# A hybrid attention trunk on one core: rows copied to all partitions by DRAM transfers instead of selector matmuls

## The chip, the cores and the metric

The program runs on one core of a Trainium2 chip. The metric is the device time of one execution in microseconds (us). The engines are PE (TensorE; PEld is its weight load), DVE (VectorE), ACT (ScalarE), POOL (GpSimd) and SP (SyncE, which here only issues DMA transfers). Each engine works through its own queue in order and waits for semaphores of the others.

## What is computed

Two layers of a trunk on a sequence of 1024 tokens of width 1024, all in float32. Each layer normalises its input, projects it (`h @ w_in`, 9180 columns) and runs three branches on the result: sparse attention (DSA, the best 256 keys of each query by an index score, 8 heads), stick-breaking attention (8 heads) and a chunked mLSTM (4 heads of 128). The gated sum of the branches goes through `w_out` and is added to the input.

Two pieces matter here. The first is the decays of the mLSTM (reduced from the reference):

```python
b = jnp.cumsum(lfb, axis=-1)
log_d = jnp.where(tril, b[..., :, None] - b[..., None, :] + ib[..., None, :], -jnp.inf)
log_inter = b + m_prev[..., None]
m_row = jnp.maximum(jnp.max(log_d, axis=-1), log_inter)
w_intra = jnp.exp(log_d - m_row[..., None])
w_inter = jnp.exp(log_inter - m_row)
s = jnp.einsum('bhtd,bhsd->bhts', qb, kb) * w_intra
num = einsum(s, vb) + w_inter * einsum(qb, c_mem)
c_mem = decay * c_mem + einsum(w_upd, kb, vb)
```

The second is the keys of DSA: of the 64 entries of a key the first 16 are the rotated `k_rope`, the same for all heads, and the other 48 are `c_kv @ w_uk`.

## The kernel before

`body` (L614) does not issue instructions but logs them. `Plan.run` then sets every engine's order by simulating the program with a table of costs (L82 to 91, `cost`), buffers and priorities, and `Plan.emit` issues the instructions in that order at L533, which is why all rows of the profile name that line. A small edit in `body` can therefore move rows anywhere. Buffers of 520 or 1032 columns per partition (classes `half`, 21, and `slab`, 35; two halves may share a slab) and eight PSUM banks are handed out by the planner too. In rows, `t` is a buffer, `s` one that lies in a shared slab, `d` a DRAM buffer.

A float32 product is three passes of F32R matmuls over a high and a low part of each operand (`PASSES`). A layer runs in this order: projections and index scores; the mLSTM; the stick-breaking attention; DSA; the merge. Two things run beside it. The merge gates (`AHEAD`, L1038) are projected early and fill PE between other work, in the buffers `fill` and PSUM banks `psf`. The top-k search (`tk_bit`) is a chain of 32 rounds, put between other steps by `tick` (L944). A round (`count`, L951) counts over six score tiles: DVE does the tiles of 384, 512 and 640 columns, ACT those of 768, 896 and 1024, and three small DVE operations on 128x6 make the next threshold out of the six counts.

The mLSTM works on chunks of 128 tokens, 4 heads (`h`), two halves (`th`) of four chunks each. Heads 0 and 2 project values and gates for two heads and are longer. For a head, PE transposes the keys, and DVE multiplies them by the update weights into `kw` (L1200 to 1207). Then for each half:

- `selm(h)` (L1212) is a matmul with a column of `sel_ml`, copied along the free axis, as the stationary operand and `pk[th]` as the moving one. `pk[th]` holds high and low parts of eight rows (decay `rr_`, inter-chunk weight `wi`, four heads each); the product adds the two parts of one row and copies it to all 128 partitions. The next matmul (L1213) adds the causal mask `m_ml` in bf16. ACT takes the exponential with a bias per partition, from PSUM.
- PE multiplies keys and queries, DVE multiplies the product by the exponential into `Wt`.
- `selm(4 + h)` (L1225) copies the row `wi` to all partitions; DVE multiplies the queries by it into `qs`.
- For each chunk PE computes `Wt` x values and adds `qs` x state; from `kw` x values (128x129, two passes of float32) and the old state DVE makes the new state, with the factor `dec` (L1249).

The rows of `pk` are written to DRAM and read back in another layout (L1116 to 1128). `dec` (L1134 to 1140) is made by 8 four-column selector matmuls per layer.

In DSA, `dsa_k` (L1465) computes the keys of a pair of heads, 128x512 for each half: three passes `w_uk` x `c_kv` with zeros in the 16 rotary rows, and a fourth matmul (L1478) that adds the rotary rows with the selector `sel_kr` and the tile `krs[th]`, which is loaded from `kr_d` once per layer. `stack_k` (L1291) splits the result into high and low parts, two tiles per half (ACT casts, DVE subtracts, 64x512 each). `logits` (L1384) uses them.

Of the kernel before, what the change touches and what calls it, by code (L numbers as in the profile page):

```python
# [613 lines left out]
def body(log, tiles, caps, x_in, w_in, w_uk, w_uv, kvn, conv_w, ib, fb, mln, w_br, w_out, nrm, fnrm,  # L614
# [50 lines left out]
    sel_kr = const([128, 128], F32R, "sel_kr")  # L665
    zer = const([128, 48], F32, "zer")
    V.memset(zer, 0.0)
    for e in range(2):
        V.tensor_tensor(sel_kr[:, 64 * e:64 * e + 16], ident[:, 0:16], ident[:, 16:32], ALU.add)
        V.tensor_copy(sel_kr[:, 64 * e + 16:64 * e + 64], zer)  # L670
    sel_ml = const([128, 8], F32R, "sel_ml")
    for j in range(8):
        k = (j % 4) + 8 * (j // 4)
        V.tensor_tensor(sel_ml[:, j:j + 1], ident[:, k:k + 1], ident[:, k + 4:k + 5], ALU.add)
# [10 lines left out]

    def selm(j):
        return sel_ml[:, j:j + 1].to_broadcast([128, 128])
# [109 lines left out]
    for l in range(DEPTH):  # L797
# [317 lines left out]
        hl = half(F32R)  # L1115
        pkd = dram([4, 32, 128], F32R)  # L1116
        for q, src in ((0, rr_), (2, wi)):
            split(src, hl[0:32, q * 128:q * 128 + 128], hl[0:32, q * 128 + 128:q * 128 + 256])
        for q in range(4):
            SY.dma_start(f(pkd[q]), f(hl[0:32, q * 128:q * 128 + 128]))  # L1120
        pk = []
        for th in range(2):
            k = half(F32R)
            pk.append(k)
            G.memset(f(k[:, :512]), 0.0)
            for q in range(4):
                SY.dma_start(f(k[4 * q:4 * q + 4, :512]).rearrange("h (c t) -> h c t", c=4),
                             f(pkd[q, 16 * th:16 * th + 16, :]).rearrange("(c h) t -> h c t", h=4))
# [5 lines left out]
        pd = pst("tr")  # L1134
        for h in range(4):
            for th in range(2):
                PE.matmul(pd[:, h * 8 + th * 4:h * 8 + th * 4 + 4], selm(4 + h),
                          pk[th][:, 127:512:128], start=True, stop=True)
        dec = small([128, 4, 8], name="dec", bufs=1)
        V.tensor_copy(dec, pd[:, 0:32].rearrange("p (h c) -> p h c", h=4))  # L1140
# [3 lines left out]
        for h in range(4):  # L1144
# [63 lines left out]
            Cst = None  # L1208
# [224 lines left out]


        ckh, ckl = [], []
        krs = []
        for th in range(2):
            c = half()
            SY.dma_start(c[:, :512], ckvT_d[:, th * 512:th * 512 + 512])
# [265 lines left out]
```

## Time and profile before

| what | us |
|---|---|
| time, median of 3 runs | 2734.28 |
| lowest and highest of the 3 | 2730.94, 2734.89 |
| the profiled execution's own time | 2734.7 |
| its span, from first to last instruction | 2732.9 |
| PE busy | 2690.6 |
| DVE, ACT, POOL busy | 1670.8, 1474.7, 1109.0 |

A group row of the profile gives count, busy time, mean length of one and the idle time ahead of it with what ended that. Matmuls overlap, so the price of one is the distance from start to start, which a merged timeline row gives as its length by its count. A timeline row merges neighbouring rows and bears the shape of the first. The wait in square brackets is idle time ahead of the first instruction of the row.

### The profile page before, as it was taken

To read this page: it belongs to the slowest core of one execution; us is meant where nothing else is said; L and a number is where in the kernel's file an instruction comes from. 1 tells how busy PE (TensorE), PEld (TensorE's weight loads), DVE (VectorE), ACT (ScalarE), POOL (GpSimd) and SP (SyncE) were. 2 spreads that over 40 slices of the span, in tenths; PEclk is the share of its full clock that TensorE was granted. 3 is DMA by queue.
4 is the path that set the end of the run, shared out by engine and by line. 5 is a ranking of instruction groups with operands and counts; after the bars stand their busy time and mean duration, and the time that the engine had idled before them with its cause. 6 is when DMAs were issued, how large, how long until landed. Compare 5 with 4: busy or idle time off the path is not lost.

```text
span 2732.9 us, 43639 instructions
## 1 busy us (share of the span) xinstructions
PE 2690.6 (98%) x15658; PEld 2306.7 (84%) x15666; DVE 1670.8 (61%) x3964; ACT 1474.7 (54%) x2961; POOL 1109.0 (41%) x1481
## 2 busy tenths in 40 slices
PE   8999999999999999999899999999999999999998
PEld 7888878888888888889898888888888888888898
DVE  5828788666686663424447287896676776624244
ACT  4637763545567766512236277735555577764131
POOL 4323333334253433455433233442342444334654
PEclk9999999999999999999999999999999999999999
DMA  4302112112132215745313022122121322246462
GB/s 131 97 16 80 37 57 83 39 55 82 31 103 61 78 54 177 243 143 206 104 41 109 24 62 62 51 67 66 39 74 33 102 64 77 61 167 231 161 206 77
DMA packets 251149, 249.53 MB, mean 91 GB/s; under 512 B 22378, under 2 KB 201908, under 8 KB 250932
## 3 DMA queue, kind: packets, MB, share of 16 engines
q1 hardware_dynamic: 250932, 246.75, 28.5%
q8 instruction: 123, 2.02, 0.3%
q14 instruction: 94, 0.77, 0.1%
HBM read 184.37 MB, written 62.32 MB: 90 GB/s over the span
## 4 chain that ended last, share of the span: by engine, by line
PE 52%; ACT 3%; DVE 2%; issue 1%; DMA 1%; POOL 1%; SPq 0%; POOLq 0%; DVEq 0%; ACTq 0%
PE t L533 52%; ACT t L533 2%; DVE t L533 1%; POOL t L533 1%; ACT s L533 1%; DMA d<-t 0%; DMA t<-in_w_in_dram 0%; ACT L533 0%; DVE s L533 0%; SPq L533 0%; DMA t<-d 0%; POOLq L1701 0%; DVEq L533 0%; ACTq L533 0%; POOLq L533 0%
## 5 line engine op out<-in xcount | busy, mean ns | idle before, releaser
L533 PE MATMUL t<-t,t 128*128 128x512 f32 (+5 forms) x15466 | 2669.2, 336 | 34.7 <-DVE t L533 29.2
L533 PEld LDWEIGHTS t<-t,t 128*128 128x128 f32 x15330 | 2271.0, 184 | 394.9 <-DVE t L533 41.2
L533 POOL TENSOR_TENSOR t<-t,t 128x256 fp32r<-128x256 f32 (+4 forms) x1092 | 875.7, 830 | 1178.8 <-ACT t L533 470.9
L533 DVE TENSOR_TENSOR t<-t,t 128x512 f32<-128x512 f32 (+14 forms) x1514 | 757.4, 532 | 691.0 <-ACT t L533 498.3
L533 ACT CAST t<-t 128x512 fp32r<-128x512 f32 (+6 forms) x1073 | 563.9, 569 | 520.3 <-PE t L533 238.7
L533 ACT ACTIVATE t<-t 128x512 f32<-128x512 f32 (+4 forms) x704 | 350.8, 593 | 339.6 <-PE t L533 216.3
L533 ACT ACTIVATE t<-t,t 128x768 bf16<-128x768 f32 (+10 forms) x352 | 279.1, 813 | 26.4 <-DVE t L533 18.3
L533 ACT COPY t<-t 64x256 f32<-64x256 f32 (+4 forms) x294 | 109.4, 377 | 267.1 <-PE t L533 262.9
L533 DVE TENSOR_TENSOR_SCAN t<-t 128x256 f32<-128x256 f32 (+10 forms) x144 | 210.5, 1473 | 6.5 <-ACT t L533 6.2
L533 DVE SCALAR_TENSOR_TENSOR t<-t,t,t 128x512 f32<-128x512 f32 (+8 forms) x214 | 162.3, 777 | 28.4 <-DMA d<-t 11.6
L533 POOL TENSOR_SCALAR t<-t 64x512 fp32r<-64x512 f32 x128 | 85.1, 666 | 194.2 <-ACT t L533 157.7
L533 ACT ACT_TABLE_LOAD x111 | 142.4, 1283 | 25.9 <-PE t L533 13.4
L533 POOL TENSOR_SCALAR t<-t,t 128x256 f32<-128x256 f32 (+7 forms) x128 | 95.4, 754 | 138.4 <-DVE t L533 126.1
L533 DVE TENSOR_SCALAR_CACHE_REDUCE t<-t,t 128x512 bf16<-128x512 f32 (+2 forms) x173 | 128.3, 768 | 0.9
L533 DVE TENSOR_TENSOR s<-s,t 128x512 f32<-128x512 f32 x70 | 51.5, 737 | 96.3 <-PE t L533 96.2
L533 DVE CUSTOM_DVE_ANT_0 t<-t,t 128x512 f32<-128x512 f32 (+3 forms) x160 | 92.6, 591 | 20.9 <-PE t L533 17.6
L533 DVE TENSOR_SCALAR t<-t 128x1 f32<-128x1 f32 (+5 forms) x324 | 59.1, 188 | 24.0 <-ACT t L533 21.6
L533 PE MATMUL t<-s,t 128*128 128x512 f32 (+1 forms) x192 | 62.3, 379 | 0.0
L533 DVE RECIPROCAL t<-t 128x1 f32<-128x1 f32 (+1 forms) x144 | 23.0, 163 | 56.1 <-ACT t L533 55.2
L533 DVE TENSOR_TENSOR t<-t 128x1 f32<-128x1 f32 (+9 forms) x234 | 53.0, 238 | 4.7 <-POOL t L533 2.3
L533 ACT ACTIVATION_READ_ACCUMULATOR t<-t,t 128x1 f32 x280 | 52.9, 189 | 0.0
L533 ACT ACTIVATE s<-t,t 128x896 bf16<-128x896 f32 (+2 forms) x40 | 41.6, 1041 | 15.0 <-DVE s L533 14.5
(37 smaller groups left out, 417.4 us busy)
## 6 DMA issues: line engine op xcount, KB each, us to landing
t<-in_w_in_dram SPq DMA_DIRECT2D x192, 256.0 KB
d<-t SPq DMA_DIRECT2D x134, 256.0 KB
t<-d SPq DMA_DIRECT2D x128, 256.0 KB
t<-in_w_in_dram SPq DMA_DIRECT2D x44, 512.0 KB
s<-d SPq DMA_DIRECT2D x76, 256.0 KB
d<-t SPq DMA_DIRECT2D x130, 128.0 KB
t<-in_w_branch_dram SPq DMA_DIRECT2D x32, 512.0 KB
t<-in_w_out_dram SPq DMA_DIRECT2D x32, 512.0 KB
```

Of the source, the lines that this page charges most:

```text
L533: fn(*args, **kw)
```

## The change

- The mLSTM's rows `rr_` and `wi` go to DRAM as they are (two stores of 32x128 in place of four stores of high and low parts). For each head and half, two transfers (`row`) read a row of 4 x 128 values from there into all 128 partitions, 512 bytes a piece, 256 KB a transfer; 32 in the two layers.
- GpSimd adds the mask `m_ml` to the decay row, two operations of 128x256 for each head and half. ACT takes the exponential from this row. DVE multiplies the queries by the other row, from SBUF instead of PSUM. The state's decay is the last column of each chunk in that row; `dec` is gone.
- DSA's keys are computed by three passes, and `stack_k` splits them without the rotary part. Then four transfers of 16x512 for each pair and half write the rotary rows' high and low parts from `kr_d` into the two tiles. `krs` and its memsets are gone.
- The selectors `sel_ml`, `sel_kr` and their set-up are gone.

```diff
--- before.py
+++ after.py
@@ -662,16 +662,6 @@
     cs = const([128, NB, 16], F32, "cs")
     neghalf = const([128, 1], F32, "neghalf")
     V.memset(neghalf, -0.5)
-    sel_kr = const([128, 128], F32R, "sel_kr")
-    zer = const([128, 48], F32, "zer")
-    V.memset(zer, 0.0)
-    for e in range(2):
-        V.tensor_tensor(sel_kr[:, 64 * e:64 * e + 16], ident[:, 0:16], ident[:, 16:32], ALU.add)
-        V.tensor_copy(sel_kr[:, 64 * e + 16:64 * e + 64], zer)
-    sel_ml = const([128, 8], F32R, "sel_ml")
-    for j in range(8):
-        k = (j % 4) + 8 * (j // 4)
-        V.tensor_tensor(sel_ml[:, j:j + 1], ident[:, k:k + 1], ident[:, k + 4:k + 5], ALU.add)
...
-
-    def selm(j):
-        return sel_ml[:, j:j + 1].to_broadcast([128, 128])
 
...
@@ -1112,32 +1099,23 @@
         S.activation(wi, rr_, AF.Exp, bias=mpc)
         S.activation(wu, ii, AF.Exp, bias=rr_[:, 127:128])
         S.activation(en, ml, AF.Exp, scale=-1.0)
-        hl = half(F32R)
-        pkd = dram([4, 32, 128], F32R)
-        for q, src in ((0, rr_), (2, wi)):
-            split(src, hl[0:32, q * 128:q * 128 + 128], hl[0:32, q * 128 + 128:q * 128 + 256])
-        for q in range(4):
-            SY.dma_start(f(pkd[q]), f(hl[0:32, q * 128:q * 128 + 128]))
-        pk = []
-        for th in range(2):
-            k = half(F32R)
-            pk.append(k)
-            G.memset(f(k[:, :512]), 0.0)
-            for q in range(4):
-                SY.dma_start(f(k[4 * q:4 * q + 4, :512]).rearrange("h (c t) -> h c t", c=4),
-                             f(pkd[q, 16 * th:16 * th + 16, :]).rearrange("(c h) t -> h c t", h=4))
+        row_d = dram([2, 32, 128])
+        for q, src in enumerate((rr_, wi)):
+            SY.dma_start(row_d[q], src)
+
+        def row(q, h, th):
+
+            r = half()
+            a = row_d[q, 16 * th + h:16 * th + h + 1, :]
+            SY.dma_start(r[:, :512].rearrange("p (c t) -> p c t", c=4),
+                         bass.AP(tensor=a.tensor, offset=a.offset, ap=[[0, 128], [512, 4], [1, 128]]))
+            return r
+
         p = pst("tr")
         for q, src in enumerate((ii, wu, en)):
             PE.transpose(p[:, q * 32:q * 32 + 32], src, ident[:32, :32])
         mlc = small([128, 3, 8, 4], name="mlc", bufs=1)
         V.tensor_copy(mlc.rearrange("p q c h -> p (q c h)"), p[:, 0:96])
-        pd = pst("tr")
-        for h in range(4):
-            for th in range(2):
-                PE.matmul(pd[:, h * 8 + th * 4:h * 8 + th * 4 + 4], selm(4 + h),
-                          pk[th][:, 127:512:128], start=True, stop=True)
-        dec = small([128, 4, 8], name="dec", bufs=1)
-        V.tensor_copy(dec, pd[:, 0:32].rearrange("p (h c) -> p h c", h=4))
 
...
@@ -1206,25 +1184,26 @@
                                 mlc[:, 1, th * 4:th * 4 + 4, h, None].to_broadcast([128, 4, 128]), ALU.mult)
                 kw.append(k)
             Cst = None
+            rows_ = []
+            for th in range(2):
+                r = row(0, h, th)
+                pool_tt(r, r, m_ml.rearrange("p a b -> p (a b)"), ALU.add, 512)
+                rows_.append((r, row(1, h, th)))
             tick(2)
             for th in range(2):
-                p = pst("lg")
-                PE.matmul(p, selm(h), pk[th][:, :512], start=True, stop=False)
-                PE.matmul(p, identb, m_ml.rearrange("p a b -> p (a b)"), start=False, stop=True)
+                rrow, wrow = rows_[th]
                 Wt = half()
                 for t in range(4):
                     c = th * 4 + t
-                    S.activation(Wt[:, t * 128:t * 128 + 128], p[:, t * 128:t * 128 + 128], AF.Exp,
+                    S.activation(Wt[:, t * 128:t * 128 + 128], rrow[:, t * 128:t * 128 + 128], AF.Exp,
                                  bias=mlc[:, 0, c, h:h + 1])
                 p = pst("lg")
                 for t in range(4):
                     PE.matmul(p[:, t * 128:t * 128 + 128], cv[1, th][:, t * 128:t * 128 + 128],
                               cv[0, th][:, t * 128:t * 128 + 128], start=True, stop=True)
                 V.tensor_tensor(Wt[:, :512], Wt[:, :512], p, ALU.mult)
-                p = pst("lg")
-                PE.matmul(p, selm(4 + h), pk[th][:, :512], start=True, stop=True)
                 qs = half()
-                V.tensor_tensor(qs[:, :512], cv[0, th][:, :512], p, ALU.mult)
+                V.tensor_tensor(qs[:, :512], cv[0, th][:, :512], wrow[:, :512], ALU.mult)
                 NUM = half()
                 nv = NUM[:, :516].rearrange("p (t c) -> p t c", t=4)
                 for t in range(4):
@@ -1246,7 +1225,8 @@
                         if c == 0:
                             V.tensor_copy(Cn, p[:, :129])
                         else:
-                            V.scalar_tensor_tensor(Cn, Cst, dec[:, h, c:c + 1], p[:, :129], ALU.mult, ALU.add)
+                            V.scalar_tensor_tensor(Cn, Cst, wrow[:, t * 128 + 127:t * 128 + 128], p[:, :129],
+                                                   ALU.mult, ALU.add)
                         Cst = Cn
...
@@ -1433,7 +1413,6 @@
 
 
         ckh, ckl = [], []
-        krs = []
         for th in range(2):
             c = half()
             SY.dma_start(c[:, :512], ckvT_d[:, th * 512:th * 512 + 512])
@@ -1441,11 +1420,6 @@
             split(c[:, :512], hi, lo)
             ckh.append(hi)
             ckl.append(lo)
-            k = half(F32R)
-            G.memset(f(k[:, :512]), 0.0)
-            for q in range(2):
-                SY.dma_start(f(k[16 * q:16 * q + 16, :512]), f(kr_d[q, :, th * 512:th * 512 + 512]))
-            krs.append(k)
...
@@ -1474,9 +1448,13 @@
             for th in range(2):
                 p = pst("mm")
                 for i, (a, b) in enumerate(PASSES):
-                    PE.matmul(p, uw[:, 128 * a:128 * a + 128], ck[b][th][:, :512], start=(i == 0), stop=False)
-                PE.matmul(p, sel_kr, krs[th][:, :512], start=False, stop=True)
-                r["k"].append(stack_k(p))
+                    PE.matmul(p, uw[:, 128 * a:128 * a + 128], ck[b][th][:, :512], start=(i == 0), stop=(i == 2))
+                k = stack_k(p)
+                for e in range(2):
+                    for q in range(2):
+                        o = 64 * (e ^ q)
+                        SY.dma_start(f(k[e][o:o + 16, :512]), f(kr_d[q, :, th * 512:th * 512 + 512]))
+                r["k"].append(k)
             return r
 
         def dsa_v(pr):
```

**DVE at head 0 of the first layer.** The second layer reads the same. The 128x384, 128x512 and 128x640 rows are a round of counts; the two TENSOR_TENSOR that read `t_1602` (before) and `t_1588` (after) make `kw`. Before:

```order
L533 TENSOR_SCALAR s_2263,t_2264<-t_1025,t_2261 128x384 [waits DMAHW4_49,DMAHW1_49,DMAHW7_49,DVE_49,Pool_49]
L533 TENSOR_SCALAR s_2272,t_2264<-t_1067,t_2261 128x512 [waits PE_49]
L533 TENSOR_TENSOR t_2283<-t_2270,t_1602 128x512 [waits PE_49]
L533 TENSOR_TENSOR t_2279<-t_2279,t_2213 128x512 [waits Activation_49]
L533 TENSOR_TENSOR t_2296<-t_2277,t_1602 128x512 [waits PE_49]
L533 TENSOR_SCALAR s_2306,t_2264<-t_1108,t_2261 128x640 [waits Activation_49]
```

After:

```order
L533 TENSOR_SCALAR s_2224,t_2225<-t_1009,t_2217 128x384 [waits DMAHW2_49,DMAHW0_49,DMAHW3_49,DVE_49,Pool_49]
L533 TENSOR_SCALAR s_2231,t_2225<-t_1051,t_2217 128x512 [waits DMAHW4_49,DMAHW1_49,PE_49]
L533 TENSOR_SCALAR s_2242,t_2225<-t_1092,t_2217 128x640 [waits DVE_49,Activation_49]
L533 TENSOR_TENSOR t_2256<-t_2240,t_1588 128x512 [waits DMAHW1_49,PE_49]
L533 TENSOR_TENSOR t_2254<-t_2254,t_2180 128x512 [waits DMAHW6_49,Activation_49]
L533 TENSOR_TENSOR t_2271<-t_2248,t_1588 128x512 [waits PE_49]
```

The count over 640 columns, which waits for ACT, stood behind both products of `kw` and now stands ahead of both.

**DVE at head 2 of the first layer**, the same steps. Before:

```order
L533 TENSOR_SCALAR s_3857,t_3858<-t_1025,t_3854 128x384 [waits DMAHW2_49,DVE_49,PE_49]
L533 TENSOR_SCALAR s_3864,t_3858<-t_1067,t_3854 128x512 [waits PE_49]
L533 TENSOR_SCALAR s_3873,t_3858<-t_1108,t_3854 128x640 [waits DVE_49,Activation_49]
L533 TENSOR_TENSOR t_3886<-t_3870,t_1602 128x512 [waits PE_49]
L533 TENSOR_TENSOR t_3884<-t_3884,t_3809 128x512 [waits Activation_49]
L533 TENSOR_TENSOR t_3897<-t_3877,t_1602 128x512 [waits PE_49]
```

After:

```order
L533 TENSOR_SCALAR t_3821,t_3822<-t_1009,t_3816 128x384 [waits DVE_49]
L533 TENSOR_TENSOR t_3801<-t_3801,t_3662 128x512 [waits Activation_49]
L533 TENSOR_SCALAR t_3837,t_3822<-t_1051,t_3816 128x512
L533 TENSOR_TENSOR t_3849<-t_3829,t_1588 128x512 [waits DVE_49,PE_49]
L533 TENSOR_TENSOR t_3842<-t_3842,t_3775 128x512 [waits DMAHW0_49,Activation_49,Pool_49]
L533 TENSOR_TENSOR t_3869<-t_3834,t_1588 128x512 [waits PE_49]
```

Here the count over 640 columns stood ahead of `kw` and now stands behind it (it follows five rows on). In head 2 of the second layer, where before the rows stood as in the first layer, they read after:

```order
L533 TENSOR_SCALAR t_18675,t_18676<-t_15865,t_18669 128x384 [waits DVE_49]
L533 TENSOR_SCALAR t_18683,t_18676<-t_15907,t_18669 128x512 [waits Pool_49]
L533 TENSOR_SCALAR t_18690,t_18676<-t_15948,t_18669 128x640
L533 TENSOR_TENSOR t_18724<-t_18711,t_16398 128x512 [waits DVE_49,PE_49]
L533 TENSOR_TENSOR t_18731<-t_18720,t_16398 128x512 [waits DVE_49,PE_49]
```

The count stays ahead of `kw` there, with no wait of its own.

**ACT around head 0 of the first layer.** The four-part 128x128 rows are the exponentials of the decays, `t_2279` (before) and `t_1990` (after) are gates, the 128x896 and 128x1024 rows counts. Before:

```order
L533 ACTIVATE t_2279<-t_2213 128x512 [waits PE_49]
L533 ACTIVATE s_2288,t_2264<-t_1232,t_2261 128x896
L533 ACTIVATE s_2298,t_2264<-t_1295,t_2261 128x1024 [waits Activation_49]
L533 ACT_TABLE_LOAD [waits PE_49]
L533 ACTIVATE t_2313<-t_2286,t_1602 128x128 [waits Pool_49]
L533 ACTIVATE t_2313<-t_2286,t_1602 128x128 x3
```

After:

```order
L533 ACTIVATE t_1962<-t_1838,t_1588 128x128 [waits DMAHW6_49,Pool_49]
L533 ACTIVATE t_1962<-t_1838,t_1588 128x128
L533 ACTIVATE t_1962<-t_1838,t_1588 128x128 [waits Pool_49]
L533 ACTIVATE t_1962<-t_1838,t_1588 128x128
L533 ACT_TABLE_LOAD [waits PE_49]
L533 ACTIVATE t_1990<-t_1947 128x512 [waits Activation_49]
```

The exponentials of the head stood behind the last gate and the counts; now the last of them stand ahead of all eight gates that the head projects, and they wait for POOL and the transfers instead of PE. In SP's queue the four transfers for head 0 stand directly ahead of the weight loads for head 1's projections.

## Rows read from the trace of the kernel before

**Rows 1.** The page: busy time by engine, granted clock of PE in 40 slices (tenths).

```profile
PE 2690.6 (98%) x15658; PEld 2306.7 (84%) x15666; DVE 1670.8 (61%) x3964; ACT 1474.7 (54%) x2961; POOL 1109.0 (41%) x1481
...
PEclk9999999999999999999999999999999999999999
```

**Rows 2.** Busy time by stretch: the mLSTM stages of both layers (x: instructions).

```profile
core 0: us, PE busy (x) PEld busy (x) DVE busy (x) ACT busy (x) POOL busy (x), PEclk, DMA share, GB/s
...
128.00:430.00 302.00, 296.74 (x1598) 252.21 (x1601) 211.77 (x563) 191.28 (x367) 114.30 (x157) 0.99 0.18 52
...
1487.00:1800.00 313.00, 308.49 (x1665) 262.54 (x1670) 224.87 (x575) 199.78 (x375) 118.83 (x162) 0.99 0.17 50
```

**Rows 3.** Timeline of PE, from 299.83 us: start, length, count, in us.

```profile
299.83 10.39 PE L533 MATMUL t<-t,t 128*128 128x512 f32 x44
```

**Rows 4.** Groups of PE instructions by shape: count | busy, mean ns | idle before.

```profile
L533 PE MATMUL t<-t,t 128*128 128x512 f32 x6936 | 1809.3, 402 | 2.3 <-POOL t L533 1.2 <-DVE t L533 1.0
...
L533 PE MATMUL t<-t,t 128*128 128x512 bf16 x8 | 3.6, 454 | 0.0
...
L533 PE MATMUL t<-t,t 128*128 128x4 f32 x16 | 2.1, 235 | 0.5 <-DMA t<-d 0.5
```

**Rows 5.** Timeline of PE: head 1, first layer; decay table, second layer.

```profile
236.31 3.88 PE L533 MATMUL t<-t,t 128*128 128x512 f32 x15
...
1487.37 4.85 PE L533 MATMUL t<-t,t 128*128 128x4 f32 x24 [0.53 <-DMA t<-d]
```

**Rows 6.** Timeline of PE and of DVE: head 2 of both layers.

```profile
347.32 6.94 PE L533 MATMUL t<-t,t 128*128 128x129 f32 x24 [3.81 <-DVE t L533]
...
345.78 0.88 DVE L533 TENSOR_SCALAR_CACHE_REDUCE s<-t,t 128x640 bf16<-128x640 f32 x1 [1.59 <-ACT s L533]
...
1717.86 8.32 PE L533 MATMUL t<-t,t 128*128 128x129 f32 x41 [2.25 <-DVE t L533]
...
1716.31 0.88 DVE L533 TENSOR_SCALAR_CACHE_REDUCE s<-t,t 128x640 bf16<-128x640 f32 x1 [1.60 <-ACT s L533]
```

**Rows 7.** Busy time by stretch just behind the two stops (columns as in 2).

```profile
347.30:354.00 6.70, 6.68 (x24) 5.79 (x25) 3.71 (x10) 4.71 (x13) 4.26 (x6) 0.53 0.00 0
...
1717.90:1722.30 4.40, 4.30 (x16) 3.33 (x17) 3.19 (x9) 2.68 (x6) 2.89 (x4) 0.62 0.00 0
```

**Rows 8.** Timeline of PE and of DVE: head 0 of both layers.

```profile
206.37 5.89 PE L533 MATMUL t<-t,t 128*128 128x129 f32 x39 [0.85 <-DVE t L533]
...
1575.60 4.62 PE L533 MATMUL t<-t,t 128*128 128x129 f32 x24 [0.85 <-DVE t L533]
...
204.83 0.88 DVE L533 TENSOR_SCALAR_CACHE_REDUCE s<-t,t 128x640 bf16<-128x640 f32 x1 [1.01 <-ACT s L533]
```

**Rows 9.** Timelines: first keys of DSA (PE, DVE); SP's issues; SP's waits.

```profile
820.73 6.50 PE L533 MATMUL t<-t,t 128*128 128x256 f32 x46
827.55 6.70 PE L533 MATMUL t<-t,t 128*128 128x512 f32 x32 [0.32 <-DVE t L533]
...
824.82 5.62 DVE L533 TENSOR_TENSOR t<-t,t 64x512 fp32r<-64x512 f32 x12
...
1483.58 1.27 SPq L533 DMA_DIRECT2D t<-d  x4
...
SPq L533 <- ACT t L533: 1389.0, 172, 76.8
```

**Rows 10.** Groups and timelines of POOL and DVE: adds, and small operations beside them.

```profile
L533 POOL TENSOR_TENSOR t<-t,t 128x256 f32<-128x256 f32 x32 | 22.9, 739 | 138.8 <-DVE t L533 138.8
...
333.80 7.01 POOL L533 TENSOR_TENSOR t<-t,t 128x256 f32<-128x256 f32 x10 [9.70 <-DVE t L533]
...
335.99 0.67 DVE L533 TENSOR_SCALAR t<-t 128x6 int32<-128x6 f32 x1
...
342.42 0.17 DVE L533 TENSOR_SCALAR t<-t 128x6 int32<-128x6 f32 x1
```

**Rows 11.** PE's waits: us in total, times, longest.

```profile
PE t L533 <- DVE t L533: 29.2, 18, 7.9
```

## The prediction

> **What bounds the kernel now.** I read the page first: TensorE (PE) is busy for 98% of the span and its granted clock is at 9 tenths or more in every slice [rows 1]. The table by stage comes next: in the two mLSTM stages, where most of the change lies, PE is busy for 296.7 of 302 us and 308.5 of 313 us, while VectorE (DVE) is busy for about 70%, ScalarE (ACT) for 64% and GpSimd (POOL) for 38% [rows 2]. So time is won only where PE has fewer columns to stream or fewer waits. The unit price comes from a stretch with nothing but 128x512 matmuls: 44 in 10.39 us, 0.236 us each [rows 3].
>
> What is not streaming in the mLSTM stages is a handful of waits for DVE, and one kind matters. In head 2, PE stops for 3.81 us (first layer) and 2.25 us (second) at the first 128x129 matmul, whose operand `kw` DVE makes [rows 6]. DVE was late because a top-k count over 640 columns stood ahead of `kw` in its queue and waited 1.59 and 1.60 us for ACT, which holds the buffer of its output [rows 6]. After each stop the granted clock is 0.53 over 6.70 us and 0.62 over 4.40 us, that is mostly the lower of the two levels, 1.2 instead of 2.4 GHz [rows 7]. So a stop costs idle time plus lost clock: 3.81 + 6.70 x 0.47 = 7.0 us, and 2.25 + 4.40 x 0.38 = 3.9 us. In head 0 the same wait is 0.85 us in either layer: there the held count stands behind `kw` [rows 8].
>
> **What leaves PE.** Of each kind [rows 4] shows what the trace has recorded (of the bf16 mask products 8 of the 16 that the code issues).
> - mLSTM: per layer 4 heads x 2 halves x 3 matmuls of 512 columns (decay row, mask, inter-chunk weight), 48 in all. Heads 0 and 2: 24 x 0.236 = 5.7 us. In heads 1 and 3 six stand in a row; the row of head 1 has 15 matmuls in 3.88 us, so six take 3.88 - 9 x 0.236 = 1.76 us, 0.29 each [rows 5]: 24 x 0.29 = 7.0 us.
> - Keys: 4 pairs x 2 halves x 2 layers = 16 x 0.236 = 3.8 us.
> - Decay table: 8 four-column matmuls per layer. In the second layer the row has 24 matmuls in 4.85 us, 16 of them with 512 columns: 4.85 - 16 x 0.236 = 1.07 us, and PE waited 0.53 us for a DMA ahead of them [rows 5]. Two layers: 2 x 1.07 + 0.53 = 2.7 us.
>
> Sum: 5.7 + 7.0 + 3.8 + 2.7 = **19.2 us**, against 17.2 if all 64 wide ones cost 0.236 us and the 16 narrow ones the 2.1 us of their group [rows 4]. I take the upper end, since it is measured in place. Less than 17.2 could leave only where PE waits anyway; that is the next term.
>
> **What is given back.** In heads 0 and 2 three of the removed matmuls stand between the transposes for `kw` and the product that needs it. There PE is already at DVE's pace (waits in [rows 6, 8]), so their 3 x 0.236 = 0.71 us become a longer wait: 4 heads x 0.71 = 2.8 us (bounds 0 and 2.8; I take 2.8). Net gain on PE: 16.4 us.
>
> **What the new order does to the held count.** The order of DVE's queue shows that the count over 640 columns that waits for ACT moves from behind both `kw` products to ahead of them in head 0, in both layers. In head 2 of the first layer it moves the other way, and in head 2 of the second layer it stays ahead but no longer names ACT. I price head 0 at the mean of the two stops, (7.0 + 3.9) / 2 = 5.4 us per layer, less the 0.85 us that it waits now: + 9.1 us. Head 2 gives back 7.0 us and about half of 3.9 us, since the counts ahead of it still run: - 9.0 us. Net + 0.1. The bounds are wide: -12.6 us if no head is held (7.0 + 3.9 + 2 x 0.85), + 9.1 us if head 0 is held and head 2 stays as it is.
>
> **What is added, and its cover.** POOL gets 32 adds of 128x256. The same shape in f32 takes 0.739 us [rows 10], so 23.6 us on an engine that is 41% busy [rows 1], less 8 memsets. In the order of ACT's queue head 0's exponentials stand many rows ahead of the transposes that open the head, where the exponentials of before followed a matmul of the head itself; so adds, exponentials and inter-chunk product end early and cost PE nothing. SP gets 68 more transfers at 1.27 / 4 = 0.32 us of issue [rows 9], 22 us on a queue that spends 1389 us waiting for ACT alone [rows 9]; behind a waiting one stand weight loads and stores. The decay rows are in SP's queue before the loads of the next weights, long before use: zero. If that cover failed, each late row would stop PE as `kw` does.
>
> For the key rows, the first pair is the tight place. Its last product starts near 822.8 us and the first logits near 833.2 us: 46 matmuls from 820.73 us, then 32 from 827.55 us, 24 of them of 512 columns ahead of the logits [rows 9]. The copies take 12 DVE rows in 5.62 us from 824.82 us, four of them for these keys' first half and four for the second [rows 9]. Eight transfers take 8 x 0.32 = 2.5 us to issue. From the issue of the last of four transfers (1483.58 + 1.27 = 1484.85 us) to the matmul that waited for it at 1487.37 us it is 2.5 us [rows 5, 9]. That makes 824.8 + 3.7 + 2.5 + 2.5 = 833.5 us if all eight are needed, but the first logits need only the first two: zero, at most about 2 us in each layer. The other pairs have more matmuls between.
>
> **The sum.** Profiled execution 2734.7 us (span 2732.9 and 1.8 around it), 0.4 above the median. 2734.7 - 19.2 + 2.8 + 0.1 = 2718.4; against the median of 2734.28 that is 2718.
>
> **A rule weighed.** A DVE operation on 128x6 takes 0.67 us while POOL runs ten operations of 128x256 without a break, and 0.17 us when POOL is idle [rows 10]. The Trainium skill, page "SBUF — State Buffer", section "SBUF: two separate sides", says that DVE and GpSimd share a port pair as an exclusive lock, and that a DVE operation with two SBUF inputs is blocked for the whole of a GpSimd operation that reads SBUF. The trace agrees as far as these rows go, and the rule speaks against this change. What it would do is the third rival below.
>
> **Rivals, worked out.**
> 1. No head is held: the exponentials leave ACT's queue at the heads, so counts and buffers come free sooner. 2734.3 - 19.2 - 12.6 = 2702.5. For it: head 2 of layer one in the new order. Against: head 0.
> 2. Held at head 0 and at head 2: 2734.3 - 19.2 + 2.8 + 9.1 = 2727. For it: the same row of counts stands ahead of `kw` in the second layer's head 2.
> 3. Adds lock DVE out. 32 adds and 16 products that now read two SBUF operands: if each add stops a DVE operation that PE waits for, 32 x 0.739 = 23.6 us, 2742. Against: the adds stand early, where nothing on DVE is urgent. It decides against the change only if nearly all of them fall in a head's chain.
> 4. Slower by the hold: at all eight heads of the two layers DVE reaches `kw` late at the price of 7.0 us: 8 x 7.0 - 12.6 = 43.4 more, 2734.3 - 16.4 + 43.4 = 2761. It outweighs the gain, and 0.2%, from five held heads on ((16.4 + 5.5 + 12.6) / 7.0 = 4.9). For it: rearranged queues, two held heads today. Against: only heads 0 and 2 hold counts ahead of `kw` today.
> 5. Key rows land late in the first pair of each layer: 2 x (2 us and about as much in clock) = 8, 2726.
> 6. The matmuls leave and PE idles as long, because every head waits for DVE anyway: 2734. Against: the stages have 5.3 and 4.5 us without PE work [rows 2], so PE is not paced by DVE.
>
> **How the numbers follow.** Forecast 2718, 0.48; rival 1, 0.18; rival 2, 0.13; rival 3, 0.05; rival 4, 0.06; rival 5, 0.06; rival 6, 0.04. The forecast alone spans 2712 (nothing given back, the new order a few us kinder) to 2726 (17.2 leaves, head 2 gives back half as much). Rivals 3 and 4 lie above 2733, and a tail of rival 1 below 2702: range 2702 to 2733. This kernel's measurement tells about 0.2%, 5.5 us, from no change, so faster is below 2728.8 us and slower above 2739.7 us. Faster: forecast 0.46, rival 1 0.18, rival 2 0.08, rival 5 0.04, together 0.76. Slower: rivals 3 and 4, most of them, 0.10. The rest, 0.14, is no change.
>
> **What would show it.** PE has 80 matmul rows fewer; PE's busy time is about 17 to 19 us less; the wait of the first 128x129 matmul in head 0 grows to 2 us and more with a granted clock below 0.7 behind it, and that in head 2 of the first layer is under 1 us. Waits of PE for DMA stay under 2 us in total. The forecast is wrong if PE's wait for DVE, 29.2 us in all now [rows 11], changes by more than 10 us, or if PE waits for transfers at the first logits.

## The result and the profile after

The changed kernel takes **2709.8 us** (median of four executions, 2709.5 to 2712.6) against 2734.2 us of before on the same chip: a ratio of 0.9917, interval 0.9905 to 0.9929, or 22.7 us less (2734.28 x 0.0083); the two medians lie 24.4 us apart. The profiled execution's span falls from 2732.9 to 2708.2 us. The forecast was 2718, with a range from 2702 to 2733.

The busy line and the clock line of the page of after, which answer to [rows 1]:

```profile
PE 2668.8 (99%) x15586; PEld 2290.3 (85%) x15586; DVE 1675.4 (62%) x3945; ACT 1476.5 (55%) x2955; POOL 1131.6 (42%) x1505
...
PEclk9999999999999999999999999999999999999999
```

PE's weight loads fall from 15666 to 15586, that is by the 80 rows which the change takes out. (Matmul rows fall by 72 only: before, eight of the mask products were not recorded.) PE is busy for 21.8 us less, POOL for 22.6 us more.

The mLSTM stages in the table of busy time by stretch, columns as in [rows 2] (the second layer comes earlier now, so its stretch is shifted):

```profile
128.00:430.00 302.00, 300.86 (x1664) 257.95 (x1663) 223.75 (x569) 195.05 (x367) 120.41 (x167) 1.00 0.25 65
1480.00:1790.00 310.00, 309.02 (x1722) 266.05 (x1721) 229.50 (x586) 195.62 (x370) 126.22 (x177) 1.00 0.22 63
```

PE was idle for 5.3 us of the first stretch before and is for 1.1 us now; its granted clock there rose from 0.99 to 1.00. PE's waits in all, columns as in [rows 11]:

```profile
PE t L533 <- DVE t L533: 22.4, 14, 7.9
PE t L533 <- POOL t L533: 4.2, 11, 0.8
PE t L533 <- ACT t L533: 3.1, 6, 1.0
```

Waits for DVE fell by 6.8 us; there is no row for a DMA. Now the heads. First the place where the prediction had put the new stop, head 0, in the timelines of PE (both layers) and of DVE (first layer):

```profile
202.72 2.13 PE L533 MATMUL t<-t,t 128*128 128x129 f32 x15 [0.98 <-DVE t L533]
...
1558.34 2.13 PE L533 MATMUL t<-t,t 128*128 128x129 f32 x15 [0.98 <-DVE t L533]
```

```profile
196.23 0.59 DVE L533 TENSOR_TENSOR t<-t,t 128x6 f32<-128x6 f32 x1 [1.55 <-ACT s L533]
...
201.18 0.88 DVE L533 TENSOR_SCALAR_CACHE_REDUCE s<-t,t 128x640 bf16<-128x640 f32 x1 [1.60 <-ACT s L533]
...
201.98 1.89 DVE L533 TENSOR_TENSOR t<-t,t 128x512 f32<-128x512 f32 x3
```

The count over 640 columns does stand ahead of `kw` (the products at 201.98 us), and it is held for 1.60 us, as the order said. Yet PE stops for 0.98 us only. The 0.85 us of [rows 8] were not the same wait: the single records of PE (one for each instruction, which a timeline merges) show that the first 128x129 matmul of head 0 of before ran at 203.00 us without a wait, and the one at 206.37 us waited for a DVE product behind the held count. In DVE's timeline of before, the first product of `kw` and that product:

```profile
201.53 0.69 DVE L533 TENSOR_TENSOR t<-t,t 128x512 f32<-128x512 f32 x1
...
205.63 0.68 DVE L533 TENSOR_TENSOR t<-t,t 128x512 f32<-128x512 f32 x1
```

So head 0 had a stop by the hold before too, at another product; now the stop is at `kw`. PE's granted clock behind the stop of after is 1.00, its upper level of 2.4 GHz (table by stretch):

```profile
202.70:209.40 6.70, 6.68 (x51) 6.35 (x52) 6.63 (x20) 6.02 (x16) 1.42 (x2) 1.00 0.00 0
```

Over as many microseconds behind the 3.81 us stop it was 0.53 [rows 7]. In head 2 both stops are gone. In DVE's timeline of after the count of the first layer follows `kw`; in the second layer the last count ends at 1692.4 us, unheld, and DVE then waits for PE's transposes:

```profile
339.33 1.88 DVE L533 TENSOR_TENSOR t<-t,t 128x512 f32<-128x512 f32 x3
...
342.78 0.88 DVE L533 TENSOR_SCALAR_CACHE_REDUCE t<-t,t 128x640 bf16<-128x640 f32 x1
...
1691.50 0.88 DVE L533 TENSOR_SCALAR_CACHE_REDUCE t<-t,t 128x640 bf16<-128x640 f32 x1
...
1694.93 1.53 DVE L533 TENSOR_TENSOR t<-t,t 128x512 f32<-128x512 f32 x3 [2.55 <-PE t L533]
```

The 24 matmuls of 512 columns ahead of the first logits of DSA wait as long as before, 0.32 us, and for DVE [rows 9]; the logits behind them start at 836.25 us without a wait. The row is cut by the end of its window:

```profile
830.60 5.57 PE L533 MATMUL t<-t,t 128*128 128x512 f32 x23 [0.32 <-DVE t L533]
```

### The profile page after: what moved, and what is told of

It is laid out like the page before. It is cut to its first block, busy times and chain, and to the rows that moved or that the text cites. A ratio compares the mean times of both kernels' runs of the same rounds, so it can differ in the third digit from the quotient of the medians.

```text
span 2708.2 us, 43662 instructions
## 1 busy us (share of the span) xinstructions
PE 2668.8 (99%) x15586; PEld 2290.3 (85%) x15586; DVE 1675.4 (62%) x3945; ACT 1476.5 (55%) x2955; POOL 1131.6 (42%) x1505
## 5 line engine op out<-in xcount | busy, mean ns | idle before, releaser
L533 PE MATMUL t<-t,t 128*128 128x512 f32 (+4 forms) x15336 | 2647.5, 335 | 31.6 <-DVE t L533 22.4
L533 DVE TENSOR_TENSOR t<-t,t 128x512 fp32r<-128x512 f32 (+12 forms) x1481 | 747.1, 535 | 659.7 <-ACT t L533 473.0
L533 ACT CAST t<-t 128x256 fp32r<-128x256 f32 (+5 forms) x1068 | 564.8, 568 | 539.3 <-PE t L533 259.4
L533 ACT ACTIVATE t<-t,t 128x768 bf16<-128x768 f32 (+8 forms) x328 | 291.5, 894 | 30.4 <-DVE t L533 25.6
L533 DVE SCALAR_TENSOR_TENSOR t<-t,t,t 128x512 f32<-128x512 f32 (+6 forms) x199 | 166.0, 856 | 25.5 <-POOL t L533 10.3
L533 POOL TENSOR_SCALAR t<-t,t 128x128 f32<-128x128 f32 (+7 forms) x128 | 94.8, 750 | 147.7 <-DVE t L533 132.9
L533 DVE TENSOR_SCALAR_CACHE_REDUCE t<-t,t 128x512 bf16<-128x512 f32 (+4 forms) x197 | 145.0, 766 | 1.1
L533 DVE CUSTOM_DVE_ANT_0 t<-t,t 128x512 f32<-128x512 f32 (+3 forms) x160 | 92.7, 591 | 24.4 <-PE t L533 16.6
L533 DVE TENSOR_SCALAR t<-t 128x1 f32<-128x1 f32 (+6 forms) x324 | 62.4, 200 | 27.0 <-ACT t L533 25.0
L533 DVE TENSOR_TENSOR t<-t 128x1 f32<-128x1 f32 (+6 forms) x224 | 52.6, 244 | 5.2 <-POOL t L533 2.4
L533 PE MATMUL t<-s,t 128*128 128x512 f32 (+2 forms) x154 | 49.8, 375 | 0.0
L533 DVE TENSOR_SCALAR t<-t,t 128x512 f32<-128x512 f32 (+12 forms) x78 | 40.0, 523 | 15.4 <-ACT t L533 13.1
```

What stands on the lines that cost most here:

```text
L533: fn(*args, **kw)
```

## Where the time went

To split the 24.7 us of span I added up, over all PE rows of a trace, the distance from each start to the next. A row's price is the median distance of its shape (232 ns for 512 columns, 118 for 256, about 110 for 128 and less); the rest is **excess**: idle time, lost clock, slow neighbours. "Heads" is from the first to the last 128x129 matmul of a layer, both layers. Eight mask products that some traces lack are counted among the columns.

| us | columns | excess in heads | excess elsewhere | sum |
|---|---|---|---|---|
| before | 2637.1 | 15.9 | 64.1 | 2717.1 |
| after | 2620.5 | 2.8 | 69.0 | 2692.3 |
| difference | -16.6 | -13.1 | +4.9 | -24.8 |
| said ahead | -19.2 | +2.9 | 0 | -16.3 |

So the columns left about as said. The heads lost their stops, which had not been said; a part of that came back elsewhere. Among what grew are PE's waits for POOL (1.3 us before, 4.2 after) and for ACT (1.4 and 3.1). Three questions follow: what made the stops, what do the added transfers and adds cost, and is the keys part worth its 3.8 us?

## Experiments

Each is timed against the kernel before on the same chip; where two experiments are compared, it is by their ratios to before.

### One part of the change at a time

e1 keeps the mLSTM part and gives DSA its selector and `krs` back; e2 is the reverse.

```diff
...
-                    PE.matmul(p, uw[:, 128 * a:128 * a + 128], ck[b][th][:, :512], start=(i == 0), stop=(i == 2))
-                k = stack_k(p)
-                for e in range(2):
-                    for q in range(2):
-                        o = 64 * (e ^ q)
-                        SY.dma_start(f(k[e][o:o + 16, :512]), f(kr_d[q, :, th * 512:th * 512 + 512]))
-                r["k"].append(k)
+                    PE.matmul(p, uw[:, 128 * a:128 * a + 128], ck[b][th][:, :512], start=(i == 0), stop=False)
+                PE.matmul(p, sel_kr, krs[th][:, :512], start=False, stop=True)
+                r["k"].append(stack_k(p))
```

> The mLSTM part of the change alone; the rotary rows are added to the keys by the selector matmul as before. Theory A (columns and stops): 48 wide and 16 narrow matmuls leave (about 14 us) and the two stops of head 2 (10.9 us) with them, so about 2711 us; the keys' part is then worth 0 to 2 us. Rival B (every removed column counts at 0.236 us wherever it is, and the stops are a matter of the order drawn): 2734 - 11.3 - 2.7 = 2720 us. In DSA, PE's wait and lost clock should be as before.

Measured: 2714.3 us (2712.0 to 2715.2), ratio 0.9931, 0.9916 to 0.9946, half-way between the two expectations (2711 and 2720 us are ratios of 0.9916 and 0.9949). The stops of head 2 are gone, as the first had it. The group of 128x129 matmuls on buffers `t` among PE's groups by shape, of e1 (count | busy, mean ns | idle before); the group of before stands further below, with 8.2 us:

```profile
L533 PE MATMUL t<-t,t 128*128 128x129 f32 x264 | 43.6, 277 | 2.0 <-DVE t L533 2.0
```

> The keys' part alone; the mLSTM is as before, its two stops in head 2 too. By the columns 16 x 0.236 = 3.8 us leave: 2730.5 us. The rival, that DSA gives back as much in new small waits (by start-to-start distances the trace of after has some 4 us more of them in DSA than before), gives 2734 us or a little more.

Measured: 2739.6 us (2736.0 to 2741.3), ratio 1.0024, 1.0013 to 1.0034: **slower**, where 3.8 us of columns leave. Its timeline of PE, at head 2 of both layers:

```profile
348.47 69.24 PE L533 MATMUL t<-t,t 128*128 128x129 f32 x357 [4.19 <-DVE t L533]
...
1720.16 5.06 PE L533 MATMUL t<-t,t 128*128 128x129 f32 x20 [2.32 <-DVE t L533]
```

Here both stops are as before. So the mLSTM part took them away, not the keys part; and by the ratios the mLSTM part is worth 18.9 us on the kernel before, and 29.3 us on e2 (1.0024 to 0.9917), each with some 4 us of uncertainty. What e2 lost is taken up again below.

### The held count: a buffer of its own

The count writes an output that nobody reads, into a pool buffer (`junk`) that ACT may still hold. e5 and e6 give DVE's counts a fixed one, in the kernel before and in the changed one.

```diff
+    junk_v = const([128, 640], BF16, "junk_v")
...
-                junk = half(BF16, 1040)
+                junk = half(BF16, 1040) if i in TK_ACT else junk_v
```

> The kernel before, in which VectorE's three counts of a top-k round write their unused result into a buffer of their own instead of one that is handed out among all; so the count over 640 columns no longer waits for the buffer that ScalarE holds. If that held count makes the two stops of head 2: both are below 1 us, and the time is about 2734 - 10.9 = 2723 us, up to 2727 us. If VectorE is late there for another reason (the chain of rounds itself): the stops stay, 2734 us.

> The same edit on the changed kernel. It has no such stop any more, only 0.98 us in head 0 of either layer, so theory A expects 2708 to 2710 us; more than 3 us either way would be the order drawn anew in other stages.

Measured: e5 2723.9 us (2722.5 to 2724.1), ratio 0.9965, 0.9951 to 0.9979, 9.6 us less than before. e6 2705.5 us (2703.4 to 2706.1), ratio 0.9898, 0.9883 to 0.9913; that is 5.2 us below after, with about as much uncertainty, where 0 to 2 us had been expected. By the reckoning of the table above about 1 us of it lies in the heads and 4 us elsewhere. In e5's timelines of DVE and PE, head 2 of the first layer has neither a held count (337.78 us) nor a stop (one unbroken row of PE):

```profile
337.78 0.88 DVE L533 TENSOR_SCALAR_CACHE_REDUCE t<-t,t 128x640 bf16<-128x640 f32 x1
...
337.73 12.49 PE L533 MATMUL t<-t,t 128*128 128x512 f32 x79
```

The group of 128x129 matmuls, first of before, then of e5, has lost its idle time:

```profile
L533 PE MATMUL t<-t,t 128*128 128x129 f32 x352 | 58.4, 284 | 8.2 <-DVE t L533 7.8
```

```profile
L533 PE MATMUL t<-t,t 128*128 128x129 f32 x344 | 52.9, 277 | 0.2
```

One edit of the counts' output thus removes the stops without touching a column: the held count is their cause. How much the change itself had done to it is seen in the groups of DVE: the counts over 640 columns whose output lies in a shared slab (`s`), first of before, then of after (in e5 and e6 no such row is left):

```profile
L533 DVE TENSOR_SCALAR_CACHE_REDUCE s<-t,t 128x640 bf16<-128x640 f32 x12 | 10.6, 879 | 11.8 <-ACT s L533 11.7
```

```profile
L533 DVE TENSOR_SCALAR_CACHE_REDUCE s<-t,t 128x640 bf16<-128x640 f32 x4 | 3.5, 880 | 5.6 <-ACT s L533 5.6
```

Twelve such counts waiting 11.8 us became four waiting 5.6 us; eight of the twelve make up nearly all of the 11.8. The pair e5 and e6 also gives the change without any hold: from 0.9965 to 0.9898, 18.3 us, with some 5.6 us of uncertainty from the two intervals. By its steps, columns less give-back, the prediction had 16.4 for that.

### The same kernels in another order

Any edit makes the planner draw a new order. To see whether the stops hang on one order, e7 and e8 raise an allowance that the planner adds to each handover between engines, in the kernel before and in the changed one.

```diff
-EXTRA = 0.0
+EXTRA = 2.0
```

> The kernel before with 2 ns added to every latency between engines in the planner's table, which changes no instruction and only draws another order. If the stops of head 2 belong to the code: they stay (4 to 11 us together) and the time is 2734 us within 5. If they belong to the order drawn: they go, about 2724 us.

> The same 2 ns on the changed kernel: another order of the same instructions. Theory A: no stop over 1.5 us in any head, and the time within 5 us of 2709.8, the rest being the merge, the change of layers and DSA. Rival B (the gain beyond the columns was luck): up to 2718 us, with a stop of 2 us or more in a head.

Measured: e7 2735.3 us (2733.8 to 2737.5), ratio 1.0008, 0.9998 to 1.0017; e8 2707.1 us (2705.3 to 2707.8), ratio 0.9904, 0.9890 to 0.9919. The stop of head 2 in the first layer stays in e7's order (timeline of PE), and ahead of it in DVE's timeline the same held count; the second fence is the stretch behind the stop in the table by stretch:

```profile
347.01 8.92 PE L533 MATMUL t<-t,t 128*128 128x129 f32 x38 [3.39 <-DVE t L533]
...
345.47 0.88 DVE L533 TENSOR_SCALAR_CACHE_REDUCE s<-t,t 128x640 bf16<-128x640 f32 x1 [1.60 <-ACT s L533]
```

```profile
347.00:353.70 6.70, 6.69 (x25) 5.75 (x25) 4.63 (x13) 4.38 (x11) 2.83 (x4) 0.52 0.11 27
```

In e8 the group has:

```profile
L533 PE MATMUL t<-t,t 128*128 128x129 f32 x264 | 43.6, 277 | 2.2 <-DVE t L533 2.1
```

In the second layer of e7, 0.73 and 0.51 us are left of the 2.25 us, so how long a stop is does hang on the order. That there are long ones does not, in these two orders each: with the selectors and the shared buffer the first layer has one, without the selectors neither layer has.

### The columns back, unread

e4 is the changed kernel with 48 products of 512 columns at the places of those removed from the heads. They multiply other operands and nobody reads them.

```diff
+                p = pst("lg")
+                for i in range(2):
+                    PE.matmul(p, mov(0, i, th)[:, :128], mov(0, 2, th), start=(i == 0), stop=(i == 1))
...
+                p = pst("lg")
+                PE.matmul(p, mov(0, 0, th)[:, :128], mov(0, 2, th), start=True, stop=True)
```

> The changed kernel with three matmuls of 512 columns put back at each place where the selectors and the mask stood, 48 in all; nobody reads their results and they wait for nothing but a bank. The decays still come by transfer. If the columns alone are worth 0.236 us each: 2709.8 + 11.3 = 2721 us, and what then is missing to the kernel with the mLSTM of before (e2) is the price of its waits. If PE had room for them in its waits: 2710 to 2714 us.

Measured: 2730.0 us (2728.1 to 2732.9), ratio 0.9991, 0.9981 to 1.0: 20 us more than after (0.9991 against 0.9917), where the columns alone make 48 x 0.236 = 11.3, and beyond both expectations. Its busy line, PE's waits for ACT, the group of 128x129 matmuls and, in the timeline, the longest of the new stops:

```profile
PE 2683.0 (98%) x15634; PEld 2303.0 (84%) x15634; DVE 1677.8 (62%) x3945; ACT 1498.4 (55%) x2973; POOL 1113.5 (41%) x1505
```

```profile
PE t L533 <- ACT t L533: 8.3, 10, 2.3
```

```profile
L533 PE MATMUL t<-t,t 128*128 128x129 f32 x264 | 42.1, 277 | 0.7 <-DVE t L533 0.7
```

```profile
1250.77 46.68 PE L533 MATMUL t<-t,t 128*128 128x256 f32 x393 [2.27 <-ACT t L533]
```

PE is busy for 14.2 us more; waits for ACT grew by 5.2 us, and the stop at 1250.77 us lies far behind the mLSTM, where no column was put back. That these waits are the new order's doing is argued from their place; no run separates them. The stops in the heads did not come back with the columns. So the columns on PE were not what made DVE late; among what differs still, the exponentials now need no matmul of the head and leave ACT's queue early. That this is the link is argued from the order, since no run moved the exponentials alone.

### The adds on POOL, twice

```diff
                 pool_tt(r, r, m_ml.rearrange("p a b -> p (a b)"), ALU.add, 512)
+                pool_tt(r, r, m_ml.rearrange("p a b -> p (a b)"), ALU.add, 512)
```

> The changed kernel with every mask add on GpSimd done twice (minus 2e30 where it was minus 1e30), so 32 operations of 128x256 more, 23.6 us of GpSimd. If the adds are covered: within 3 us of 2709.8. If they lock VectorE out where TensorE waits for it: up to 23.6 us more, 2733 us.

The mask is added a second time; nothing else differs in the code. Measured: 2705.6 us (2704.6 to 2712.6), ratio 0.9906, 0.9891 to 0.9921: not slower than after. The busy line of e3:

```profile
PE 2669.8 (98%) x15586; PEld 2291.9 (85%) x15586; DVE 1681.2 (62%) x3945; ACT 1481.0 (55%) x2959; POOL 1144.0 (42%) x1537
```

32 more adds, 12.4 us more of POOL, 5.8 us more of DVE, and no more time: by the ratios it is 3.0 us less than after, with some 5 us of uncertainty. Rival 3 would have had 23.6 us once more.

### Is the keys part worth anything?

e9 is e1 with the counts' own buffer, e10 is e2 with it, e11 is e2 with the planner's allowance of e7, and e12 joins e6 and e8. Each edit is shown above.

> The mLSTM part of the change alone (keys still added by the selector on PE), with the count's unread output in a buffer of its own. To be set against the whole change with that buffer (e6, 2705.5 us), from which it differs by the keys part alone. Theory 1, the keys part is worth the columns that leave, 3.8 us: 2709. Theory 2, as in e2 against before, the rotary transfers cost some 5 us more than they save: 2699 to 2701. Theory 3, the keys part is worth nothing and the differences of some us either way are the order that the planner draws: within 5 us of 2705 with either sign.

> The keys part alone, on the kernel before, with the count's unread output in a buffer of its own. To be set against e5 (before with that buffer, 2723.9 us). Theory 1: 2720. Theory 2: 2729 to 2731. Theory 3: within 5 us of 2724, either sign. In the heads of the mLSTM no stop over 1.5 us in any case, since this buffer removes the held count.

> The keys part alone, with the planner's extra allowance per edge at 2.0 in place of 0.0, which draws another order. To be set against e7 (before at 2.0, 2735.3 us). Theory 1: 2731. Theory 2: 2740 to 2742. Theory 3: within 5 us of 2735, either sign.

> The whole change with the count's own buffer and the allowance at 2.0: another draw of the fastest kernel so far. If the held count is gone by the buffer already and the rest is the draw, it lies within 4 us of 2705.5 (e6); if 2.0 helps by itself as it seemed to in e8 against after (2707.1 against 2709.8), 2702 to 2703.

Measured: e9 2716.0 us (2714.7 to 2718.0), ratio 0.9941, 0.9925 to 0.9958; e10 2719.3 (2719.1 to 2720.7), 0.9952, 0.9937 to 0.9967; e11 2738.7 (2737.3 to 2743.8), 1.0025, 1.0014 to 1.0036; e12 2705.5 (2703.3 to 2708.4), 0.9901, 0.9886 to 0.9916. e10 came out as its theory 1 had it and e12 as its first expectation; e11 lies between theories 2 and 3, and e9 outside all three of its own. Five pairs now differ by the keys part alone:

| without, with the keys part | ratios | difference, us | columns, us | excess elsewhere, us |
|---|---|---|---|---|
| before, e2 | 1, 1.0024 | +6.6 | -3.7 | +10.2 |
| e7, e11 | 1.0008, 1.0025 | +4.6 | -3.8 | +6.4 |
| e1, after | 0.9931, 0.9917 | -3.8 | -3.7 | -1.0 |
| e5, e10 | 0.9965, 0.9952 | -3.6 | -3.8 | -1.4 |
| e9, e6 | 0.9941, 0.9898 | -11.8 | -3.6 | -6.3 |

The columns leave in every pair, by the 3.8 us that had been said. The rest swings from -6 to +10 us with the order. By the intervals each difference in time has some 3 us (first row) to 6 us (last row) of uncertainty; the first and the last row are clear of nothing, the second barely, the third and fourth are not. Of the theories none held alone: two pairs are at theory 1, two go the way of theory 2 (the second of them lies within theory 3's 5 us too), and in e9 and e6 the gain is three times theory 1 and beyond theory 3's 5 us. The mean of the five is -1.6 us, with a scatter too wide to tell it from nothing or from -3.8. What exactly the order costs in e2 stays open: its PE waits 4.2 us for POOL where before waits 1.3, but so does PE of the changed kernel. Some 4 of the 10.2 us lie in the last merge, behind all work on keys: there PE of e2 stops for 2.34 us for ACT at 2619.49 us, and PE of before does not. The gain of the last row has the same source turned round: some 5 of its 6.3 us are excess in the last merge of e9, where PE stops for 1.71 us at 2658.14 us; PE of e6 does not. What else grew in e2 is spread over many places.

The group of 128x129 matmuls once more, e9, e10, e11 and e12 in turn:

```profile
L533 PE MATMUL t<-t,t 128*128 128x129 f32 x264 | 41.4, 275 | 0.0
```

```profile
L533 PE MATMUL t<-t,t 128*128 128x129 f32 x344 | 52.6, 276 | 0.0
```

```profile
L533 PE MATMUL t<-t,t 128*128 128x129 f32 x352 | 55.3, 282 | 8.1 <-DVE t L533 7.9
```

```profile
L533 PE MATMUL t<-t,t 128*128 128x129 f32 x264 | 41.5, 275 | 0.4 <-DVE t L533 0.4
```

The idle time of that group is 7.5 to 8.7 us in the four kernels that keep selectors and shared buffer (before, e2, e7, e11), 0.7 to 2.2 us in those whose exponentials follow no selector any more but whose buffer is shared (after, e1, e3, e4, e8), and at most 0.4 us with the counts' own buffer (e5, e6, e9, e10, e12). The excess in the heads, by the table's reckoning, is 14.6 to 15.9 us in the first class and 0.8 to 3.0 us in all others; elsewhere it lies between 64.1 and 76.1 us with no such pattern. e6 is the fastest with e12: the change and the buffer together, 1.0% below before.

## The prediction, step by step

- **What bounds the kernel: right.** PE stayed at 98 to 99% in every run. What moved the time was its columns and its waits.
- **What leaves PE, 19.2 us: the right rows, 2.6 us too high.** At median distances the 80 rows are worth 16.6 us. I had taken the upper end because it was "measured in place": 0.29 us a product in heads 1 and 3, and 1.07 us of the decay row per layer. Such a price holds neighbours' slowness too, which is the heads' excess. The lower end that the prediction worked out, 17.2, was the better one.
- **What is given back, 2.8 us: not found.** It rested on PE being at DVE's pace at `kw` in heads 0 and 2, but at head 0 of before `kw` came without a wait, as shown above. With the hold gone altogether, the 128x129 matmuls wait 0.2 us in e5 with the selectors as cover and 0.1 us in e6 without. The idle time in head 0 of after comes from the hold: it goes with the buffer.
- **The held count, net +0.1: this is the step that failed.** "I price head 0 at the mean of the two stops, (7.0 + 3.9) / 2 = 5.4 us per layer." The count did move to head 0 and was held for 1.60 us. But the stop was 0.98 us with no clock lost, in either layer, and it came in the place of the 0.85 us at another product, so that head 0 lost 0.13 us in all. And head 2 of the second layer gave back all of its 3.9 us, not half: its counts are over before the transposes. Idle and clock by the hold together are thus 0.26 - 7.0 - 3.9 = -10.6 us, not +0.1.

Why the price of one hold was not that of the other can be read from DVE's timeline of before, at head 2 of the first layer:

```profile
342.21 0.17 DVE L533 TENSOR_TENSOR t<-t,t 128x6 f32<-128x6 f32 x1 [2.54 <-ACT s L533]
...
346.58 2.48 DVE L533 TENSOR_TENSOR t<-t,t 128x512 f32<-128x512 f32 x4
```

There the single records of PE show the first transposes for `kw` from 340.9 to 341.3 us. Then the round *begins*: it waits for ACT's sum until 342.21 us, and its three small operations, three counts and the hold all lie between the transposes and `kw` at 346.58, 5.3 us. In head 0 of after the round began at 196.23 us and the first transposes ran from 199.8 to 200.3 us: all but 0.9 us of the hold and one count was over, and `kw` followed 1.7 us behind. So a stop's price is not the hold's length and not a neighbour's stop; it is what is left of the round when the operand is there. The order showed only that the counts stand ahead of `kw`, not when the round starts. A bound from 0 to 7.0 for head 0 was the honest one, and the near end had a reason, which the prediction gave under rival 1: the exponentials that leave ACT's queue let counts and buffers come free sooner.

- **What is added: right.** POOL's adds cost nothing, once (22.6 us of busy time against 23.6 less 8 memsets said) or twice (e3). No wait of PE for a DMA is left, so no key row came late; POOL's adds of after wait 6.9 us for loads, in three waits, but PE's 128x129 matmuls do not feel it: of the 2.1 us that they wait, 2.0 are the two stops behind the held count. Rival 5 falls, as do rival 3 by e3 and rival 4 by the groups above. The reckoning for the first keys took the row of 12 in [rows 9] for twelve copies of 64x512, but a row bears the shape of its first: the four copies of these keys run from 823.78 to 827.40 us, so there was about 1 us more room than reckoned.
- **The rule weighed.** The port lock in the Trainium skill, page "SBUF — State Buffer", section "SBUF: two separate sides", would have made e3 slower if a locked DVE operation stood on PE's path. It did not. The row of 0.67 us in [rows 10] reads one operand; the operation behind it in the trace of before, which reads two, took 0.65 us beside the adds and 0.17 us at 342.62 us. On average the 64 operations on 128x6 that convert to int32 took 250 ns before, 296 after and 298 in e3. So they did get longer with the change, but no longer still with the adds doubled; that the adds are the cause is not shown.
- **The sum.** 2718 against 2710: the columns erred by +2.6, the heads by -16.0 and the rest by +4.9 us, which makes -8.5 (-8.2 by the medians). The number came closer than the steps, by luck: two errors of the other sign took 7.5 us off the 16.0, without which the time would have been about 2702, at the very edge of the range. The result lies half-way between the forecast and rival 1 (2702.5). Rival 1's mechanism, no head held at a price, is nearly what the trace shows; its missing 7 us are columns over-priced and excess elsewhere. Rivals 2 and 6 fall: no head 2 stops, and PE does not idle instead.
- **What would show it.** Of the signs named ahead, the 80 rows, the head 2 of the first layer without a stop and PE's waits for DMA under 2 us came true; PE's busy time fell by 21.8, not 17 to 19; the wait of 2 us and a clock below 0.7 in head 0 did not come. Neither sign of being wrong came either: PE's waits for DVE fell by 6.8 us, under the 10 us that were named, though the step on the held count failed. The clock that the two stops had cost (3.1 and 1.7 us) is not in that number.

## What to carry to other kernels

An output that nobody reads still needs a buffer, and if it comes from a pool, an engine off the bound can be held there and stop the one on it: a fixed buffer took 9.6 us off the kernel before, about half of the 18.3 us that the change brings where nothing is held. Price a stop by what the queue has left to do when its operand arrives, in this place, and not by a stop elsewhere. Where a planner redraws the order at each edit, a part worth 4 us must be tried in several orders before its sign is believed.

## What the runs showed that was not expected

- What a stop costs in clock does not follow from its length. Stops of 3.81 us (before) and 3.39 us (e7) left PE's granted clock at 0.53 and 0.52 over the next 6.70 us, nearly as costly again as the stop; behind e2's 4.19 us it was 0.75 over as long. Stops of 2.25 us (before) and 2.32 us (e2) left 0.62 and 0.61 over 4.40 us, but stops of 2.34 us (e2, at 2619.49 us) and 2.27 us (e4) left 1.00 over 6.70 us, as did the 0.98 us of after. What decides it is open.
- PE's excess outside the heads, which no edit aimed at, lay anywhere between 64.1 and 76.1 us. From after to e8, where nothing but the order differs, it fell by some 4 us. A new order alone can thus hide or double what one part of this change is worth.
